# Attention weights times V as high and low fp32r parts on 128 array columns, with masks and one product on GpSimd

## The chip, the cores and the metric

The kernel runs on one core of a Trainium2 chip. The metric is the device time of one execution in microseconds. The engines are named as in the profile: PE is TensorE, DVE is VectorE, ACT is ScalarE, POOL is GpSimd, SP issues most of the DMAs. PEld is the weight load of a matmul, which runs beside the matmul ahead of it.

## The reference

Two layers on 512 tokens of width 1024, everything in float32. Layer 0 mixes by stick-breaking attention with 16 heads of 64 columns, layer 1 by a gated linear recurrence; a squared-ReLU MLP follows each. The change touches the attention alone:

```python
# q, k are RMS-normalised per head; s < t throughout
z = einsum('bhqd,bhkd->bhqk', q, k) * scale
causal = s < t
log_stay = where(causal, log_sigmoid(-z), 0.0)
log_between = cumsum(log_stay, axis=3, reverse=True) - log_stay
weights = where(causal, exp(log_sigmoid(z) + log_between), 0.0)
out = einsum('bhqk,bhkd->bhqd', weights, v)
```

So the weight of key s for query t is sigmoid(z[t,s]) times the product of sigmoid(-z[t,j]) over all j between s and t.

## The kernel before

Activations live transposed, 1024 features in eight tiles of 128 partitions by 512 tokens. Most matrix products are made exact enough by splitting both operands into a high fp32r part and a low remainder and adding three products (high by high, high by low, low by high). Weights come in slabs of 1 MB: two raw tiles `wr` from HBM, ACT casts each to the high part `wh`, DVE subtracts to get the low part `wl`. There are three `wr` buffers, two pairs `wh`, `wl`.

The attention goes by four groups of four heads. For each group the q, k and v projections (`gemm_x`, 96 products of 256 columns each, tile `ps_mm`) run on PE, and the heads of the group run while the next group's projections fill PE. In the last group the filler is the output projection (`gemm_w`, products of 512 columns). The order on PE is written by the program at build time: the class `Line` holds a clock that adds a cost per matmul, a main task (projections) and up to three live tasks (`prepare_pair`, two `head`s); a task yields the planned microseconds until it may go on, from the table `LAG`. The other engines' orders come from a scheduler that follows priorities; instructions wait for each other by semaphores.

A head has four query blocks T = 0 to 3, block T with T + 1 key blocks of 128. `z_of(T)` makes logits `z` on PE; ACT writes `sn` = sigmoid(-z) (two buffers) and `sg` = sigmoid(z); a DVE scan turns `sn` into the running product from the diagonal back; a DVE multiplication joins `sg` and the shifted `sn`. `turn(T)` transposes the blocks on PE into PSUM (`pa`); ACT and DVE bring them to SBUF as `at`, DVE multiplying the diagonal block by the constant `before`, which is the causal mask. `apply(T)` multiplies `at` by the V columns of the head in f32, 64 array columns, one product per key block, ten products per head, into `po`. `po` is one PSUM bank (pool tag `av`, one buffer) that two heads of a pair share, one in the lower and one in the upper 64 partitions. When both are done `split_out` makes the high and low part of the pair's output.

At the start, tile `ps_tr` holds the first k projection; its weights are the second slab.

Of the kernel before, what the change touches and what calls it, by code (L numbers as in the profile page):

```python
# [16 lines left out]
P = 128  # L17
# [13 lines left out]
def level_columns(H, skip):  # L31
# [27 lines left out]
def trunk(  # L59
# [20 lines left out]
    wp = ctx.enter_context(tc.tile_pool(name="wp", bufs=2))  # L80
    ap = ctx.enter_context(tc.tile_pool(name="ap", bufs=2))
# [3 lines left out]
        "P": 16, "Q": 16, "X5": 2, "R4": 4, "B": 2, "qT": 13, "sn": 2, "AT": 3, "sq": 2, "bc": 1,  # L85
# [4 lines left out]
    def sb(tag, shape=(P, S), dt=F32, name=None):  # L90
        return ap.tile(list(shape), dt, tag=tag, bufs=BUFS[tag], name=name or tag)
# [77 lines left out]
    rows = sb("AT", (40, P), name="rows")  # L169
# [6 lines left out]
    def gain(layer, j, kt):  # L176
# [10 lines left out]
    before = cp.tile([P, 2 * P], F32, name="before")  # L187
# [7 lines left out]
    nc.vector.memset(before, 1.0)  # L195
    nc.gpsimd.affine_select(
        out=before[:, P:], in_=before[:, P:], pattern=[[1, P]], compare_op=ALU.is_gt,
        fill=0.0, base=0, channel_multiplier=-1,
    )
    def late_constants():  # L200
        nc.vector.tensor_mul(gqk, gq, gk)
# [45 lines left out]
    def slab_halves(spec):  # L247
# [5 lines left out]
        def load(a):  # L253
            raw = wp.tile([P, h, nc_], F32, tag="wr", bufs=3, name="wr")
# [161 lines left out]
    def attention(norm):  # L416
# [74 lines left out]
        for g in range(4):  # L491
# [27 lines left out]
            vs = []  # L519
            for pair in range(2):  # L520
                shared = {"po": None}
# [4 lines left out]
            V = sb("B", (P, TT, SLAB), name="V")  # L526
            for hf in range(2):
                p = ps("mm")
                for u in range(2):
                    yield from gemm_x(p[:, u * SLAB : (u + 1) * SLAB], wsl, 2 * hf + u, acts)  # L530
                for u in range(2):
                    t = 2 * hf + u
                    nc.scalar.activation(
                        out=V[:, t, :], in_=p[:, u * SLAB : (u + 1) * SLAB], func=AF.Copy,
                        scale=r[:, t : t + 1],
                    )
            vs.append(V)
        return outs, heads

    live = {"sg": 0}  # L540
# [28 lines left out]
    def head(ready, vs, pair, j, shared, outs, slot):  # L569
# [3 lines left out]
        hc = (2 * pair + j) * SB_DH  # L573
# [6 lines left out]
        def z_of(T):  # L580
# [14 lines left out]
            nc.vector.tensor_tensor(  # L595
# [3 lines left out]
        at = [None] * TT  # L599

        def turn(T):
            W = (T + 1) * P
# [3 lines left out]
            at[T] = sb("AT", name="at")  # L606
            lead = W - P if T > 1 else 0
            if lead:
                nc.scalar.copy(at[T][:, :lead], p[:, :lead])
            nc.vector.tensor_mul(at[T][:, lead:W], p[:, lead:W], before[:, 2 * P - (W - lead) :])  # L610

        def apply(T):
            if shared["po"] is None:
                shared["po"] = ps("av", name="po")
            o = blk(shared["po"], T)[j * SB_DH : (j + 1) * SB_DH, :]
            for b in range(T + 1):
                mm(o, vs[0][:, b, hc : hc + SB_DH], blk(at[T], b), b == 0, b == T)

        for step in LAG["head"]:
            if isinstance(step, float):  # L620
                yield step
            else:
                kind, T = step
                while kind == "a" and not vs:
                    yield 0.5
                {"z": z_of, "t": turn, "a": apply}[kind](T)
                if step == ("t", TT - 1):
                    live["sg"] -= 1
        if j == 1:
            outs[slot] = split_out(shared["po"])  # L630
# [304 lines left out]
    def mix(sc, task, V, G, j, outs, slot):  # L935
# [30 lines left out]
        og = sb("AT", name="og")  # L966
# [11 lines left out]
    def store(m, t0, n):  # L978
# [4 lines left out]
        o = sb("AT", name="o")  # L983
# [8 lines left out]
    def trunk_steps():  # L992
# [15 lines left out]
        "raws": [wp.tile([P, KT // 2, SLAB], F32, tag="wr", bufs=3, name="wr") for _ in range(2)],  # L1008
# [17 lines left out]
    gq = sb("AT", (P, SB_DH), name="gq")  # L1026
    gk = sb("AT", (P, SB_DH), name="gk")
    nc.sync.dma_start(out=gq, in_=sb_q_gain.to_broadcast([P, SB_DH]))
    nc.sync.dma_start(out=gk, in_=sb_k_gain.to_broadcast([P, SB_DH]))
# [56 lines left out]
```

## Time and profile before

| what | value |
|---|---|
| three runs | 1322.35, 1324.25, 1326.43 us, median 1324.25 |
| profiled execution | 1325.41 us, span 1323.7 us |
| PE busy | 1300.2 us, 98% of the span |
| DVE busy | 798.7 us, 60% |
| ACT busy | 446.0 us, 34% |
| POOL busy | 80.0 us, 6% |
| f32 products of weights and V (`po`) | 320 records, start 70.8 to 286.7 us |
| HBM | 107.41 MB read, 83 GB/s over the span |

A line of the profile names the source line, the engine, the operation and its tiles (out<-in), the shapes and the count, then busy time, mean length of one in ns, and the idle time ahead of it with what ended it. One f32 matmul is recorded as two instructions, an fp32r matmul as one. In the view by order of time a row begins with its start and its length in us; matmul lengths overlap, so what a matmul costs is read from one start to the next.

### The profile page before, as it was taken

What the parts mean: (1) busy time and instruction counts of PE and PEld (TensorE: products, weight loads), DVE (VectorE), ACT (ScalarE), POOL (GpSimd) and SP (SyncE); (2) the same over time, 40 slices, a digit from 0 to 9 for tenths busy, and PEclk for the clock granted to TensorE, in tenths of its full rate; (3) what the DMA queues carried; (4) which work ended last, traced back from release to release, by engine and by line L of the source; (5) the groups of instructions that cost most, each with busy time, mean ns of one, the idle gap of its engine ahead of it and who ended that gap; (6) DMA issues with size and microseconds to landing.
All of it is one profiled execution on the core that took longest, in us unless ns stands there. A gap on an engine that the chain in (4) does not pass through costs nothing.

```text
span 1323.7 us, 17619 instructions
## 1 busy us (share of the span) xinstructions
PE 1300.2 (98%) x6993; PEld 1104.2 (83%) x6993; DVE 798.7 (60%) x1534; ACT 446.0 (34%) x756; POOL 80.0 (6%) x139
## 2 busy tenths in 40 slices
PE   7999999999999999999999999999999999999998
PEld 7989898778888888888888888888888888888887
DVE  5787687867535435345578888797764353453441
ACT  5554454544212222123333333342432221221221
POOL 0100000000000000000013222232000000000000
PEclk8999999999999999999999999999999999999999
DMA  5312121113333333333321222221333333333331
GB/s 178 108 33 65 33 68 61 49 48 96 96 96 96 96 96 96 96 96 96 96 89 47 88 64 65 64 65 64 96 96 96 96 96 96 95 96 94 97 96 48
DMA packets 110657, 110.64 MB, mean 84 GB/s; under 512 B 3848, under 2 KB 106416, under 8 KB 110576
## 3 DMA queue, kind: packets, MB, share of 16 engines
q1 hardware_dynamic: 110496, 109.22, 26.7%
q8 instruction: 55, 0.90, 0.3%
q0 software_dynamic: 80, 0.31, 0.1%
q14 instruction: 26, 0.21, 0.0%
HBM read 107.41 MB, written 2.10 MB: 83 GB/s over the span
## 4 chain that ended last, share of the span: by engine, by line
PE 84%; DVE 10%; POOL 2%; issue 2%; ACT 1%; SPq 1%; DMA 1%; DVEq 0%; POOLq 0%; ACTq 0%
PE ps_mm L151 70%; PE po L151 3%; PE ps_z L151 3%; POOL tot L812 2%; DVE sc L845 2%; PE ps_s L151 2%; DVE wl L264 2%; PE pa L155 1%; PE z L151 1%; DVE qr L826 1%; PE po_h L151 1%; PE ps_tr L151 1%; DVE sn L591 1%; DVE X L863 1%; DVE X L867 1%
## 5 line engine op out<-in xcount | busy, mean ns | idle before, releaser
L263 ACT CAST wh<-wr 128x1024 fp32r<-128x1024 f32 x198 | 199.8, 1051 | 399.8 <-PE ps_mm L151 367.8
L264 DVE TENSOR_TENSOR wl<-wr,wh 128x1024 fp32r<-128x1024 f32 x198 | 237.7, 1230 | 17.6 <-ACT wh L263 16.8
L151 PE MATMUL ps_mm<-xh,wh 128*128 128x512 f32 x592 | 232.1, 392 | 0.0
L151 PE MATMUL ps_mm<-xh,wl 128*128 128x512 f32 x592 | 230.5, 389 | 0.0
L151 PE MATMUL ps_mm<-xl,wh 128*128 128x512 f32 x592 | 230.5, 389 | 0.0
L151 PE MATMUL ps_mm<-hh,wh 128*128 128x512 f32 (+1 forms) x520 | 204.1, 393 | 0.0
L151 PE MATMUL ps_mm<-hh,wl 128*128 128x512 f32 (+1 forms) x520 | 203.6, 392 | 0.0
L151 PE MATMUL ps_mm<-hl,wh 128*128 128x512 f32 (+1 forms) x520 | 203.5, 391 | 0.0
L151 PE MATMUL ps_mm<-wh,xh 128*128 128x256 f32 x592 | 173.6, 293 | 0.0
L695 DVE TENSOR_TENSOR xT<-xT,ps_mm 128x512 f32<-128x512 f32 x63 | 43.4, 688 | 213.2 <-PE ps_mm L151 213.2
L151 PE MATMUL ps_mm<-wl,xh 128*128 128x256 f32 x592 | 167.8, 283 | 3.1 <-DVE wl L459 3.1
L151 PE MATMUL ps_mm<-wh,xl 128*128 128x256 f32 x592 | 167.6, 283 | 0.0
L151 PEld LDWEIGHTS ps_mm<-xh,wl 128*128 128x128 f32 x592 | 111.1, 188 | 23.2
L151 PEld LDWEIGHTS ps_mm<-xh,wh 128*128 128x128 f32 x592 | 111.2, 188 | 22.7
L151 PEld LDWEIGHTS ps_mm<-xl,wh 128*128 128x128 f32 x592 | 111.2, 188 | 22.5
L151 PEld LDWEIGHTS ps_mm<-wh,xh 128*128 128x128 f32 x592 | 113.5, 192 | 4.2 <-issue 3.6
L151 PEld LDWEIGHTS ps_mm<-wl,xh 128*128 128x128 f32 x592 | 113.6, 192 | 3.9 <-DVE wl L459 3.3
L151 PEld LDWEIGHTS ps_mm<-hh,wl 128*128 128x128 f32 x520 | 97.6, 188 | 22.9
L151 PEld LDWEIGHTS ps_mm<-hl,wh 128*128 128x128 f32 x520 | 97.7, 188 | 22.7
L151 PEld LDWEIGHTS ps_mm<-hh,wh 128*128 128x128 f32 x520 | 97.7, 188 | 22.6
L672 DVE SCALAR_TENSOR_TENSOR u<-ps_mm,R 128x512 f32<-128x512 f32 x60 | 41.5, 692 | 123.1 <-PE ps_mm L151 123.1
L151 PEld LDWEIGHTS ps_mm<-wh,xl 128*128 128x128 f32 x592 | 113.5, 192 | 0.0
(213 smaller groups left out, 1653.6 us busy)
## 6 DMA issues: line engine op xcount, KB each, us to landing
wr<-in_mlp_w_dram SPq DMA_DIRECT2D x128, 512.0 KB, 3.7
wr<-in_hg_w_in_dram SPq DMA_DIRECT2D x32, 512.0 KB, 3.8
wr<-in_sb_w_qkv_dram SPq DMA_DIRECT2D x22, 512.0 KB, 3.5
wr<-in_sb_w_o_dram SPq DMA_DIRECT2D x8, 512.0 KB, 3.9
wr<-in_hg_w_o_dram SPq DMA_DIRECT2D x8, 512.0 KB, 3.7
xin<-in_x_dram SPq DMA_DIRECT2D x8, 256.0 KB, 5.3
out_dram<-o SPq DMA_DIRECT2D x7, 256.0 KB, 2.3
wr<-in_sb_w_qkv_dram SPq DMA_DIRECT2D x4, 256.0 KB, 5.5
```

The lines of the kernel that those rows point to most:

```text
L151: nc.tensor.matmul(o, lhsT=lhsT, rhs=rhs, start=start, stop=stop, **kw)
L155: nc.tensor.transpose(o, in_, ident)
L263: nc.scalar.copy(hi[:, c, :], raw)
L264: nc.vector.tensor_tensor(out=lo[:, c, :], in0=raw, in1=f(hi[:, c, :]), op=ALU.subtract)
L591: nc.vector.tensor_tensor_scan(out=rev, data0=rev, data1=later[:, S - W :][:, ::-1], initial=1.0, op0=ALU.mult, op1=ALU.max,)
L672: nc.vector.scalar_tensor_tensor(out=u, in0=p, scalar=0.0, in1=norm.R, op0=ALU.max, op1=ALU.mult)
L695: nc.vector.tensor_add(xT[m], xT[m], p)
L812: nc.gpsimd.tensor_tensor(out=tots[H][:, :, None], in0=t0, in1=t1, op=ALU.mult)
L826: nc.vector.tensor_tensor(out=q1, in0=q1, in1=t0.to_broadcast([P, S // (2 * H), H]), op=ALU.mult)
L845: nc.vector.copy_predicated(out=o, mask=mask.rearrange("p (g w) -> p g w", g=g)[:, None].to_broadcast([P, 2, g, w]), data=data.rearrange(" ...
L863: nc.vector.tensor_tensor(out=o, in0=qv[:, :, :, part * H : part * H + w], in1=tv[:, :, :, part - 1, None].to_broadcast([P, TT, g, w]), op ...
L867: nc.vector.tensor_tensor(out=C, in0=B[:, :, :, H:], in1=tv[:, :, :, 1, None].to_broadcast([P, TT, g, wc]), op=ALU.mult,)
```

## The change

1. The products of weights and V take fp32r operands. `turn` writes the transposed blocks twice, `ath` (ACT cast) and `atl` (DVE remainder), for two query blocks together: half 0 holds T = 0 and 1, half 1 holds T = 2 and 3, interleaved so that one product of 256 columns serves both queries of a half. V is kept as high and low part side by side, so that a head's weight is 128 columns: the high part's sums come out in the lower 64 partitions, the low part's in the upper. Twelve products per head: eight of 256 columns, four of 128.
2. `gather`, new: each head has its own `po`; ACT copies one half of the partitions to `sum`, DVE adds the other. A pair's two heads meet in `sum`, and `split_out` reads that.
3. The causal mask is an `affine_select` on GpSimd, and the multiplication of `sg` and `sn` is on GpSimd as well. The constant `before` is gone.
4. V of a group is written in two tiles of a pool with two buffers; the main task waits for the older group's heads (`yield older`) before it makes the next V. `wr` has two buffers instead of three. The tiles `ath`, `atl` of each half have one pair of buffers (`live[half]` lets one head at a time use it).
5. `LAG` has `z`, `t`, `tt`, `a` instead of the list `head`.

```diff
-    "head": [
-        ("z", 0), 0.46, ("z", 1), 2.26, ("z", 2), 1.2, ("t", 0), ("z", 3), 1.5, ("t", 1), ("a", 0),
-        1.54, ("t", 2), ("a", 1), 1.58, ("t", 3), ("a", 2), 1.37, ("a", 3),
-    ],
+    "z": (0.46, 2.26, 1.8),
+    "t": (5.2, 5.0, 4.8, 4.8),
+    "tt": 0.7,
+    "a": (1.6, 2.1),
...
-            raw = wp.tile([P, h, nc_], F32, tag="wr", bufs=3, name="wr")
+            raw = wp.tile([P, h, nc_], F32, tag="wr", bufs=2, name="wr")
...
+            yield older
...
+                    vh, vl = v[:, u, :, 0, :], v[:, u, :, 1, :]
+                    nc.scalar.activation(out=vh, in_=src, func=AF.Copy, scale=r[:, t : t + 1])
+                    nc.vector.scalar_tensor_tensor(
+                        out=vl, in0=src, scalar=r[:, t : t + 1], in1=f(vh), op0=ALU.mult,
+                        op1=ALU.subtract,
                     )
...
-            nc.vector.tensor_tensor(
+            nc.gpsimd.affine_select(
+                out=sg[:, W - P :], in_=sg[:, W - P :], pattern=[[-1, P]], compare_op=ALU.is_gt,
+                fill=0.0, base=0, channel_multiplier=1,
+            )
+            nc.gpsimd.tensor_tensor(
                 out=sg[:, : W - 1], in0=sg[:, : W - 1], in1=sn[:, 1:W], op=ALU.mult
             )
...
+            nc.scalar.copy(ah, src)
+            nc.vector.tensor_tensor(out=al, in0=src, in1=f(ah), op=ALU.subtract)
+
+        def apply(half):
+
+            if not half:
                 shared["po"] = ps("av", name="po")
...
+            n, to = 2 * half + 2, 2 * P * (1 - half)
+            for b in range(n):
+                w = 1 if b == n - 1 else 2
+                for i, t in enumerate(at[half]):
+                    mm(
+                        shared["po"][:, to : to + w * P], vs[0][b // 2][:, b % 2, 2 * pair + j],
+                        t[:, 2 * b : 2 * b + w, :], b + i == 0, b == n - 1 and i == 1,
+                    )
+
+        def gather():
+
+            if j == 0:
+                shared["sum"] = sb("qT", name="sum")
+            po, to = [
+                t.rearrange("p (t q) -> p t q", q=P) for t in (shared["po"], shared["sum"])
+            ]
+            nc.scalar.copy(to[own], po[other][:, ::-1, :])
+            nc.vector.tensor_tensor(out=to[own], in0=po[own][:, ::-1, :], in1=to[own], op=ALU.add)
...
+        turned = 0.0
+        for T in range(TT):
+            yield from until(max(done[T] + LAG["t"][T], turned + LAG["tt"]))
+            half = T // 2
+            if T % 2 == 0:
+                while live[half]:
+                    yield 0.2
+                live[half] = 1
+            turn(T)
+            if T == 2:
+                yield from until(turned + LAG["a"][0])
+                yield from finish(0)
+            turned = line.at
+        live["sg"] -= 1
+        yield from until(turned + LAG["a"][1])
+        yield from finish(1)
+        gather()
         if j == 1:
-            outs[slot] = split_out(shared["po"])
+            outs[slot] = split_out(shared["sum"])
```

What this makes of the order shows at two places. The first is PE in group one, where the first head of a pair ends and the second goes on. Before (`po_941` belongs to both heads; `pa` are transposes, `z` logits, `ps_mm` projections):

```order
L151 MATMUL po_941<-at_999,V_576 64x128 x4
L155 MATMUL pa_1033<-ident_67,sg_845 128x128 x4
L151 MATMUL po_941<-at_1009,V_576 64x128 x3
L151 MATMUL z_1044<-kst_778,qh_780 128x256
L151 MATMUL z_1044<-kst_778,ql_782 128x256
L151 MATMUL ps_mm_918<-wh_709,xh_233 128x256
```

Now, with `po_968` the first head's bank and `po_1065` the second's:

```order
L153 MATMUL po_968<-ath_964,V_706 128x256
L153 MATMUL po_968<-atl_965,V_706 128x256
L153 MATMUL po_968<-ath_964,V_706 128x128
L153 MATMUL po_968<-atl_965,V_706 128x128
L157 MATMUL pa_1057<-ident_70,sg_848 128x128 x3
L153 MATMUL po_1065<-ath_984,V_624 128x256
L153 MATMUL po_1065<-atl_985,V_624 128x256
L153 MATMUL po_1065<-ath_984,V_624 128x128
```

The second head's first products stand three transposes behind the first head's last; before, both wrote parts of one tile. The same bank is meant by both names, so `po_1065` waits for the `gather` of `po_968`.

The second place is the end of group one on PE, where the fourth head ends. Before, with `ps_mm_1234` the next group's projection:

```order
L151 MATMUL ps_mm_1234<-wh_908,xl_280 128x256
L151 MATMUL ps_mm_1234<-wh_908,xh_156 128x256
L151 MATMUL ps_mm_1234<-wl_909,xh_156 128x256
L151 MATMUL ps_mm_1234<-wh_908,xl_157 128x256
L151 MATMUL po_1151<-at_1276,V_576 64x128 x4
L151 MATMUL ps_mm_1234<-wh_908,xh_165 128x256
```

Now the main task waits for the group's heads, and nothing else stands there (`po_1188` is the third head's bank, `po_1298` the fourth's):

```order
L153 MATMUL po_1188<-atl_1185,V_706 128x256
L153 MATMUL po_1188<-ath_1184,V_706 128x128
L153 MATMUL po_1188<-atl_1185,V_706 128x128
L157 MATMUL pa_1290<-ident_70,sg_1092 128x128 x3
L153 MATMUL po_1298<-ath_1213,V_624 128x256
L153 MATMUL po_1298<-atl_1214,V_624 128x256
L153 MATMUL po_1298<-ath_1213,V_624 128x128
L153 MATMUL po_1298<-atl_1214,V_624 128x128
L157 MATMUL pa_1303<-ident_70,sg_1092 128x128 x4
L153 MATMUL po_1298<-ath_1294,V_624 128x256
```

Projections no longer stand between the last transposes and the last products. On DVE at that place, before (`rq` belongs to the next group's norm, `wl` to a weight split):

```order
L610 TENSOR_TENSOR at_1243<-pa_1238,before_89 128x128
L228 TENSOR_SCALAR rq_a_1209<-mqk_1205 128x32
L264 TENSOR_TENSOR wl_1224<-wr_1225,wh_1223 128x1024
L610 TENSOR_TENSOR at_1253<-pa_1249,before_89 128x128
L232 TENSOR_SCALAR rq_y_1208<-rq_a_1209 128x32
L264 TENSOR_TENSOR wl_1224<-wr_1229,wh_1223 128x1024
L610 TENSOR_TENSOR at_1276<-pa_1271,before_89 128x128
```

and now, with `sum_1287` the add of `gather` for the third head:

```order
L501 SCALAR_TENSOR_TENSOR mqk_1251<-ss_711,em_428 128x16
L260 TENSOR_TENSOR wl_1270<-wr_1271,wh_1269 128x1024
L620 TENSOR_TENSOR atl_1295<-pa_1290,ath_1294 128x3x128
L643 TENSOR_TENSOR sum_1287<-po_1188,sum_1287 64x512
L224 TENSOR_SCALAR rq_a_1255<-mqk_1251 128x32
L260 TENSOR_TENSOR wl_1270<-wr_1275,wh_1269 128x1024
L228 TENSOR_SCALAR rq_y_1254<-rq_a_1255 128x32
L233 TENSOR_TENSOR rq_a_1255<-rq_y_1254 128x32
L234 SCALAR_TENSOR_TENSOR rq_a_1255<-rq_a_1255,mqk_1251 128x32
L237 SCALAR_TENSOR_TENSOR rq_y_1254<-rq_a_1255,rq_y_1254 128x32
L620 TENSOR_TENSOR atl_1295<-pa_1303,ath_1294 128x4x128
```

The add for the third head stands behind a weight split and the fourth head's remainder `atl_1295`, and the remainder of its last block behind a second split. On ACT the copies of that place stand behind a Square and a cast of weights:

```order
L422 ACTIVATE sqq_1247<-ps_mm_1106 128x512
L259 CAST wh_1269<-wr_1271 128x1024
L642 COPY sum_1287<-po_1188 64x512
L619 CAST ath_1294<-pa_1290 128x3x128
L259 CAST wh_1269<-wr_1275 128x1024
L619 CAST ath_1294<-pa_1303 128x4x128
```

The copy of `po_1188` moved in behind `sqq` and `wh`, ahead of the fourth head's cast.

More of the change, by code (lines that the diff above doesn't have):

```diff
@@ L167, in trunk @@
     nc.scalar.copy(ones_r, ones)
-    rows = sb("AT", (40, P), name="rows")
+    rows = sb("H0", (40, P), name="rows")
     nc.sync.dma_start(out=rows[0:32, :], in_=norm_gains.rearrange("l j (k p) -> (l j k) p", p=P))
@@ L572, in head @@
         kst, qh, ql = shared["k"][j], shared["q"][j], shared["ql"][j]
-        hc = (2 * pair + j) * SB_DH
+        own, other = [slice(i * SB_DH, (i + 1) * SB_DH) for i in (j, 1 - j)]
         while live["sg"] >= BUFS["X5"]:
@@ L619, in head @@
[L619 to L628, printed above, removed]
+            if T % 2 == 0:
+                at[half] = [
+                    sb(f"H{half}", (P, 4 * half + 3, P), dt=F32R, name=n) for n in ("ath", "atl")
+                ]
@@ new lines, in until @@
+        def until(t):
+            while t > line.at:
+                yield t - line.at
+        done = []
+        for T in range(TT):
+            z_of(T)
+            done.append(line.at)
+            if T + 1 < TT:
+                yield LAG["z"][T]
+        turned = 0.0
+        for T in range(TT):
+            yield from until(max(done[T] + LAG["t"][T], turned + LAG["tt"]))
+            half = T // 2
+            if T % 2 == 0:
+                while live[half]:
[6 more added lines that the diff above has]
+            turned = line.at
```

63 lines of the change are left out of this document (28 added, 35 removed).

## The prediction

> **What bounds the kernel now.** I read the page's busy times first, then a table of stretches over the attention stage, then the waits of the matmul engine, then its instructions in order of time. The first two say that TensorE (PE) carries the time:
>
> ```profile
> PE 1300.2 (98%) x6993; PEld 1104.2 (83%) x6993; DVE 798.7 (60%) x1534; ACT 446.0 (34%) x756; POOL 80.0 (6%) x139
> ```
>
> ```profile
> 53.00:111.00 58.00, 56.84 (x434) 50.95 (x433) 46.75 (x89) 30.35 (x67) 2.09 (x4) 1.00 0.18 55
> 111.00:175.00 64.00, 62.84 (x484) 57.01 (x482) 46.90 (x89) 31.33 (x67) 2.09 (x4) 1.00 0.16 50
> 175.00:233.00 58.00, 56.84 (x433) 50.97 (x432) 46.76 (x89) 30.36 (x67) 1.56 (x3) 1.00 0.16 55
> 233.00:300.00 67.00, 65.19 (x342) 50.24 (x341) 50.59 (x86) 32.99 (x66) 0.00 (x0) 0.97 0.15 48
> ```
>
> Each row is one group of four heads with its projections: length, then busy PE, weight loads, DVE, ACT, POOL. Of 247 us PE idles 1.16 + 1.16 + 1.16 + 1.81 = 5.3 us. DVE is busy 191.0 us of the same 247, so it has little room when something must be prompt. The waits of PE name the cause of most idleness, the logits waiting for ACT to free a PSUM buffer:
>
> ```profile
> PE z L151 <- ACT sg L589: 3.2, 3, 1.2
> ```
>
> A PE instruction that gets shorter here is therefore worth its length, and one that waits costs its wait, since PE's order is fixed and all later filler stands behind it.
>
> **Products of weights and V.** PE in order of time (start, length, count):
>
> ```profile
> 99.15 0.28 PE L151 MATMUL ps_mm<-wh,xl 128*128 128x256 f32 x1
> 99.36 1.09 PE L151 MATMUL po<-at,V 128*64 128x128 f32 x8
> 100.38 0.39 PE L151 MATMUL ps_mm<-wh,xh 128*128 128x256 f32 x1
> 100.60 0.28 PE L151 MATMUL ps_mm<-wl,xh 128*128 128x256 f32 x1
> 100.72 0.28 PE L151 MATMUL ps_mm<-wh,xl 128*128 128x256 f32 x1
> 100.84 0.60 PE L155 MATMUL pa<-ident,sg 128*128 128x128 f32 x4
> 101.37 0.87 PE L151 MATMUL po<-at,V 128*64 128x128 f32 x6
> 102.17 0.39 PE L151 MATMUL ps_mm<-wh,xh 128*128 128x256 f32 x1
> ```
>
> An f32 product is two records: eight take 1.02 us from start to start, six 0.80, so 0.13 each. A head has ten products, 20 records, 2.60 us; sixteen heads 41.6 us. The new head issues twelve fp32r products, eight of 256 columns and four of 128. A 256-column fp32r product takes 0.12 us (100.60 to 100.72). No row shows 128 fp32r columns. Below lies half of 0.12, if columns alone count; above lies the f32 price of two records, 0.26. I take 0.12, since each product brings a full 128-column weight load and the f32 transposes, of the same 128 by 128 shape, take 0.13 (four from 100.84 to 101.37). Then a head costs 1.44 us, all 23.0: a gain of 18.6 us (22.4 at the low end, 9.6 at the high one). The Trainium skill, "TensorE: Matmul & The Clock Gate", section "Back-to-back issue gap", gives about 81 ns per product for a stream of loads and 128-column products; it would add 2.5 us to the gain, an estimate from that page.
>
> A change of kind costs too: 0.21 instead of 0.12 before the f32 products (99.15 to 99.36), 0.22 instead of 0.12 behind them (100.38 to 100.60). By the order, 16 of the 64 runs of products of weights and V followed fp32r work, 16 x 0.09 = 1.4 us, which go; returns from f32 to fp32r fall from 72 to 69, 0.3 us. Together 1.7 us.
>
> **The wait that comes in.** One bank holds `po`. Before, two heads shared it and nobody read it between them. Now each head takes it anew, and its first product waits until ScalarE has copied one half of the last head's sums and VectorE has added the other (`gather`). Prices:
>
> ```profile
> L610 DVE TENSOR_TENSOR at<-pa,before 128x128 f32<-128x128 f32 x48 | 13.5, 285 | 17.9 <-ACT at L609 16.8 <-PE pa L155 0.9
> L560 DVE TENSOR_TENSOR kst<-pk,kst 64x512 fp32r<-64x512 f32 x16 | 11.0, 689 | 15.0 <-ACT kst L558 14.6
> L595 DVE TENSOR_TENSOR sg<-sg,sn 128x511 f32<-128x511 f32 x16 | 11.0, 687 | 0.6
> ...
> L237 DVE TENSOR_TENSOR rq_a<-rq_y 128x32 f32<-128x32 f32 x12 | 2.3, 191 | 0.3
> ```
>
> ```profile
> L558 ACT CAST kst<-pk 64x512 fp32r<-64x512 f32 x16 | 9.3, 580 | 6.1 <-PE pk L155 5.0 <-DVE kst L560 0.9
> ...
> L609 ACT COPY at<-pa 128x384 f32<-128x384 f32 x16 | 7.7, 481 | 26.9 <-PE pa L155 26.7
> ```
>
> ```profile
> 105.16 0.39 PE L151 MATMUL ps_mm<-wh,xh 128*128 128x256 f32 x1
> ...
> 105.26 0.59 ACT L340 CAST oh<-po 128x512 fp32r<-128x512 f32 x1 [3.31 <-PE po L151]
> ...
> 105.88 0.69 DVE L341 TENSOR_TENSOR ol<-po,oh 128x512 fp32r<-128x512 f32 x1 [0.38 <-ACT oh L340]
> ```
>
> The last rows give the handovers: ACT starts 0.10 behind PE, DVE 0.03 behind ACT; back to PE I put 0.05, an estimate from these two. The plain takeover is 0.10 + 0.58 (copy) + 0.03 + 0.69 (add) + 0.05 = 1.45 us, and PE has only three transposes to fill it (the order in the part on the change), 0.40: a wait of 1.05. Going through the built orders I find it five times: 5.3 us. Twice VectorE has the new head's remainder queued ahead of the add (three blocks: 0.29 for one, 0.69 for four, so 0.55); with the cast of 0.48 ahead of that, 0.10 + 0.58 + 0.48 + 0.03 + 0.55 + 0.69 + 0.05 - 0.40 = 2.1 in the fourth group, and 1.9 in the second, where the chain starts only at the transposes: 4.0 us. Two takeovers have over 2 us of filler and cost nothing.
>
> The first and third group end without filler. With the page's prices of a weight split,
>
> ```profile
> L263 ACT CAST wh<-wr 128x1024 fp32r<-128x1024 f32 x198 | 199.8, 1051 | 399.8 <-PE ps_mm L151 367.8
> L264 DVE TENSOR_TENSOR wl<-wr,wh 128x1024 fp32r<-128x1024 f32 x198 | 237.7, 1230 | 17.6 <-ACT wh L263 16.8
> ```
>
> ACT reaches the copy only behind a Square (some 0.60, as the 0.59 cast) and a cast of 1.05, and DVE has a 1.23 split and the 0.55 remainder ahead of the add: 0.10 + 0.60 + 1.05 + 1.23 + 0.55 + 0.69 + 0.05 = 4.3 from the last filler, less 0.96 of products and 0.40 of transposes, 2.9 us. Then the four-block transposes must become `ath` and `atl` with another split and five operations of 0.19 ahead: (0.95 + 1.23 + 0.69) less 1.0 of PE work, 1.85. Two such ends: 9.5 us. At the stage's end the final head's sums pass copy, add, cast, remainder, behind two splits, against nine 512-column products:
>
> ```profile
> 286.97 22.59 PE ps_mm L151 x96
> ```
>
> They last 9 x 0.235 = 2.1 us; with 0.96 of last products PE could go on at 3.1, the cast ends at 0.10 + 1.05 + 2 x 1.23 + 0.69 + 0.59 = 4.9, and its remainder 0.7 later: 2.4 us. New waits together 5.3 + 4.0 + 9.5 + 2.4 = 21.2 us. They could lie 10 lower if VectorE is early everywhere, or 5 higher if its queue is long.
>
> **GpSimd.** It takes 64 masks and 64 multiplications.
>
> ```profile
> L818 POOL TENSOR_TENSOR kk<-kk,tot 128x256 f32<-128x256 f32 x48 | 37.1, 773 | 74.6 <-PE ps_s L151 72.7
> ...
> masks.py:199 POOL TENSOR_SCALAR_AFFINE_SELECT ident<-ident 128x128 f32<-128x128 f32 x1 | 0.3, 293 | 0.1
> ```
>
> By 773 ns for 256 columns a head's 1276 columns (127, 255, 383, 511) are 3.9 us, the masks 1.2: 5 us per head of some 14, so GpSimd keeps up, and the planned time from logits to transposes, now about 5 us, holds its longest pair, 0.3 + 1.5, with 3 us for the steps ahead of it. VectorE loses the products (0.29 to 0.69, 1.9 us per head) and four mask multiplications (1.3), and gains remainders of all ten blocks (about 1.9) and the add (0.69): nearly even. But GpSimd disturbs it:
>
> ```profile
> 704.37 1.61 DVE L264 TENSOR_TENSOR wl<-wr,wh 128x1024 fp32r<-128x1024 f32 x1
> ...
> 707.44 1.23 DVE L264 TENSOR_TENSOR wl<-wr,wh 128x1024 fp32r<-128x1024 f32 x1
> ```
>
> ```profile
> 703.40 1.51 POOL L818 TENSOR_TENSOR kk<-kk,tot 128x256 f32<-128x256 f32 x2 [3.32 <-PE ps_s L151]
> ```
>
> The same split took 0.38 us more while GpSimd's pair ran. If half of 64 products do that, VectorE loses 12 us; between nothing and 24 (all of them), I put a third of 12, 4 us, on PE's path, as VectorE has 56 us free. The Trainium skill's "GPSIMD Engine Reference", section "1. Specifications", says that the two share their SBUF interface and contend where VectorE reads two SBUF operands; the rows agree, and it speaks against this move.
>
> **One raw buffer fewer.** A raw weight tile lands 3.5 us after its issue and is split within 2.3; a slab lasts 11.5 us, so the long stages lose nothing. Only the start does: the second half of slab two now waits for the second starting tile.
>
> ```profile
> 25.47 0.68 DVE L459 TENSOR_TENSOR wl<-wr,wh 128x512 fp32r<-128x512 f32 x1
> ```
>
> ```profile
> wr<-in_sb_w_qkv_dram SPq DMA_DIRECT2D x22, 512.0 KB, 3.5
> ```
>
> ```profile
> 29.57 11.52 PE ps_tr L151 x96
> ```
>
> Free at 26.15, landed at 29.7, split at 31.95; PE wants it twelve products after 29.57, at 31.1: about 1.0 us (0 to 3). The sixteen remainders of V on VectorE I cost at nothing: V is needed only after the next slab's 11.5 us; without that cover each would cost its 0.4 us. ScalarE's extra copies, some 1.5 us per head, fit into the 122 us that it idles in these stretches.
>
> **Sum.** From the profiled execution's 1325.4 us: - 18.6 - 1.7 + 21.2 + 1.0 + 4.0 = 1331.3. That execution lies 1.2 above the median, so 1330 us. About 0.3% is what a measurement can tell from no change.
>
> **Rivals.** First, relief: VectorE's queue gets short at the right places, since the product between scan and transposes leaves it. Then nothing stands ahead of the adds: each group end falls from 4.75 to about 2.5, the two late takeovers to 1.05, the stage's end to nothing, 8.8 us, and the old 5.3 us idle goes: 1316 us, faster. It decides where adds start 0.03 behind their copies everywhere. For it: the even VectorE balance; against: the built order puts splits ahead. Second, VectorE saturates: all 24 us of disturbance come, and two thirds of them fall on the path, since no room is left: 1330 - 4 + 16 = 1342, slower. It decides where DVE is busy above 95% of these stretches. Third, 128 fp32r columns cost two records: 64 x 0.14 = 9 us more, 1339.
>
> **Chances.** My forecast 0.50 (own range 1322 to 1338), relief 0.22, saturation 0.18, dear narrow products 0.10. Slower holds 0.30 of the first, saturation and 0.08 of the last: 0.56, given as 0.55; the same 0.18 and 0.02, 0.20; the rest, 0.25, faster. The range reaches from relief with cheap narrow products (1316 - 4, drawn in to 1314) to saturation and a little over, 1345.
>
> **What would show it.** Twelve `po` products near 1.44 us per head; PE waits of `po` on DVE's `sum`, 1 us and more, some ten times, and of `po` on `atl` at two group ends; DVE scans and splits above 1.22 us; one wait near 31 us. Wrong if `po` hardly waits for `sum`, or if DVE's mean times rise by half.

## The result, and the profile after

The changed kernel takes 1336.65 us (median of five runs, 1333.68 to 1340.06); the kernel before, beside it, 1324.25 (1321.63 to 1326.43). The ratio is 1.0098, 95% interval 1.0071 to 1.0124: 12.4 us slower. Forecast were 1330, 1314 to 1345, and "slower" with 0.55. The profiled execution took 1340.06 us with a span of 1338.3, against 1325.41 and 1323.7; the sums below are between these two, 14.65 us apart. One execution stands apart from all others here: the profiled one of the run e3 took 2547.24 us, with PE's products nearly twice as far from one another from end to end, so that e3 is read by its other four alone.

The page's busy times and the stretches of the four groups (length, busy PE, weight loads, DVE, ACT, POOL, then PE's granted clock, DMA share, GB/s; the first row starts at 41 us where the prediction's starts at 53, and from 41 us on PE idled the same 1.16 us before):

```profile
PE 1280.0 (96%) x6865; PEld 1108.9 (83%) x6865; DVE 806.6 (60%) x1501; ACT 466.1 (35%) x804; POOL 171.0 (13%) x266
```

```profile
41.00:111.00 70.00, 59.87 (x433) 57.14 (x433) 57.32 (x106) 38.02 (x81) 24.05 (x36) 0.89 0.24 76
111.00:175.00 64.00, 54.42 (x404) 51.62 (x404) 41.42 (x63) 32.56 (x74) 27.25 (x36) 0.93 0.11 34
175.00:233.00 58.00, 51.24 (x400) 49.42 (x400) 46.19 (x75) 33.22 (x74) 20.57 (x31) 0.97 0.18 56
233.00:300.00 67.00, 55.44 (x321) 48.95 (x320) 49.51 (x85) 34.06 (x76) 25.29 (x38) 0.87 0.15 48
```

PE was busy in nearly all of these stretches before and is not now. The column that the prediction never used is the clock: 0.87 to 0.97, where it was 0.97 to 1.00. What PE waited for in the first 330 us (total, times, longest; `atl` is the remainder of a head's own blocks):

```profile
PE po L153 <- DVE sum L643: 12.4, 7, 4.0
PE po L153 <- DVE atl L620: 7.8, 8, 1.6
PE po L153 <- DVE rq_a L224: 6.2, 2, 3.1
PE ps_mm L153 <- DVE xT L692: 4.2, 1, 4.2
...
PE po L153 <- ACT ath L619: 3.0, 3, 1.6
PE ps_mm L153 <- ACT oh L336: 1.7, 1, 1.7
```

The two waits put down to `rq_a` are takeovers as well, those at the two group ends: `rq_a` is what VectorE does right behind the add (the add starts at 102.73, `rq_a` at 103.33, PE goes on at 103.55). So the takeovers cost 12.4 + 6.2 us.

One of the plain takeovers, and what follows it, in PE's order of time (start, length):

```profile
80.93 0.38 PE L153 MATMUL po<-atl,V 128*128 128x256 f32 x1 [1.65 <-DVE atl L620]
...
81.51 0.28 PE L153 MATMUL po<-atl,V 128*128 128x256 f32 x1
81.62 0.22 PE L153 MATMUL po<-ath,V 128*128 128x128 f32 x1
81.68 0.28 PE L153 MATMUL po<-atl,V 128*128 128x128 f32 x1
81.80 0.51 PE L157 MATMUL pa<-ident,sg 128*128 128x128 f32 x3
83.35 0.58 PE L153 MATMUL po<-ath,V 128*128 128x256 f32 x1 [1.04 <-DVE sum L643]
...
84.58 0.41 PE L153 MATMUL ps_mm<-wl,xh 128*128 128x256 f32 x1
84.80 0.41 PE L153 MATMUL ps_mm<-wh,xl 128*128 128x256 f32 x1
...
90.15 0.28 PE L153 MATMUL ps_mm<-wh,xh 128*128 128x256 f32 x1
90.27 0.28 PE L153 MATMUL ps_mm<-wl,xh 128*128 128x256 f32 x1
```

The wait is 1.04 us, 2.4 us behind another of 1.65. Behind it the same 256-column product takes 0.22 us from start to start (84.58 to 84.80), at 90.15 again 0.12. The five-microsecond windows there say why:

```profile
80.00:85.00 5.00, 3.03 (x17) 2.79 (x18) 2.03 (x4) 1.06 (x2) 1.35 (x3) 0.73 0.23 79
85.00:90.00 5.00, 5.00 (x25) 4.87 (x25) 2.78 (x5) 2.80 (x8) 2.26 (x4) 0.59 0.00 0
...
100.00:105.00 5.00, 1.87 (x11) 1.67 (x11) 4.93 (x11) 2.75 (x4) 1.64 (x4) 0.78 0.28 83
105.00:110.00 5.00, 4.18 (x18) 3.49 (x17) 3.96 (x11) 1.16 (x2) 0.00 (x0) 0.50 0.38 127
```

From 85 to 90 PE is busy for all of 5.00 us, and has 25 matmul records, where the same window of before has 39 (an f32 product counts twice there): the profile's busy time hides this loss. Over the windows of 5 us from 40 to 340, PE's idle time rose from 5.3 to 40.9 us, and busy time multiplied by what the clock lacks to 1.0 rose from 1.7 to 19.7 us.

One more difference lies where nothing was said to change. Behind the attention (from the first `ps_st` to the end of the span) the kernel takes 997.3 us, before 1008.2. The groups by shape of the MLP, before and after, both from 345 to 640 us, where the changed kernel comes later and has fewer of them:

```profile
L151 PE MATMUL ps_mm<-hh,wh 128*128 128x512 f32 x222 | 87.7, 395 | 0.0
```

```profile
L153 PE MATMUL ps_mm<-hh,wh 128*128 128x512 f32 x192 | 74.7, 389 | 0.0
```

Each product that streams a Q tile (`hh`, `hl`) is 6 ns shorter by its record, 7 ns from start to start (0.2333 and 0.2267 us on the mean between 380 and 640 us). The changed kernel has a pool `gp` of its own for the tiles P and Q, which neither the change's list nor the prediction spoke of.

### The profile page after: what moved, and what is told of

Same layout as the page of the kernel before. It is cut to its first block, busy times and chain, and to the rows that moved or that the text cites. A ratio compares the mean times of both kernels' runs of the same rounds, so it can differ in the third digit from the quotient of the medians.

```text
span 1338.3 us, 17547 instructions
## 1 busy us (share of the span) xinstructions
PE 1280.0 (96%) x6865; PEld 1108.9 (83%) x6865; DVE 806.6 (60%) x1501; ACT 466.1 (35%) x804; POOL 171.0 (13%) x266
## 4 chain that ended last, share of the span: by engine, by line
PE 80%; DVE 12%; POOL 3%; issue 3%; ACT 2%; SPq 1%; DMA 0%; POOLq 0%; DVEq 0%; ACTq 0%
PE ps_mm L153 68%; PE ps_z L153 3%; DVE wl L260 2%; POOL tot L861 2%; DVE sc L894 2%; PE po L153 2%; DVE sn L593 2%; PE ps_s L153 2%; DVE qr L875 1%; PE po_h L153 1%; PE z L153 1%; PE pa L157 1%; POOL sg L601 1%; DVE X L912 1%; PE ps_tr L153 1%
## 5 line engine op out<-in xcount | busy, mean ns | idle before, releaser
L260 DVE TENSOR_TENSOR wl<-wr,wh 128x1024 fp32r<-128x1024 f32 x198 | 237.6, 1230 | 17.4 <-ACT wh L259 17.0
L153 PE MATMUL ps_mm<-hh,wh 128*128 128x512 f32 (+1 forms) x520 | 201.3, 387 | 0.0
L153 PE MATMUL ps_mm<-hh,wl 128*128 128x512 f32 (+1 forms) x520 | 200.7, 386 | 0.0
L153 PE MATMUL ps_mm<-hl,wh 128*128 128x512 f32 (+1 forms) x520 | 200.6, 386 | 0.0
L153 PE MATMUL ps_mm<-wh,xh 128*128 128x256 f32 x592 | 176.9, 299 | 0.4 <-DVE V L534 0.4
L153 PE MATMUL ps_mm<-wl,xh 128*128 128x256 f32 x592 | 170.5, 288 | 3.0 <-DVE wl L455 3.0
L153 PE MATMUL ps_mm<-wh,xl 128*128 128x256 f32 x592 | 170.4, 288 | 0.0
L153 PEld LDWEIGHTS ps_mm<-xl,wh 128*128 128x128 f32 x592 | 111.2, 188 | 22.4
L153 PEld LDWEIGHTS ps_mm<-wl,xh 128*128 128x128 f32 x592 | 116.6, 197 | 3.3 <-DVE wl L455 3.2
L153 PEld LDWEIGHTS ps_mm<-wh,xh 128*128 128x128 f32 x592 | 116.6, 197 | 2.1 <-DVE V L534 0.7
L153 PEld LDWEIGHTS ps_mm<-wh,xl 128*128 128x128 f32 x592 | 116.4, 197 | 0.0
```

What stands on the lines that cost most here:

```text
L153: nc.tensor.matmul(o, lhsT=lhsT, rhs=rhs, start=start, stop=stop, **kw)
L260: nc.vector.tensor_tensor(out=lo[:, c, :], in0=raw, in1=f(hi[:, c, :]), op=ALU.subtract)
```

## The experiments

Theory: what came in is a wait per head and, behind waits, half the clock; what came out is the work of the products and, through the new pool, 7 ns on each Q product. Rivals: VectorE paces the stage, so that any gain on PE is waited away; GpSimd's slow products make the heads late. Ratios are to the kernel before, run beside each.

**The pool, done alone and undone.** e1 is the kernel before with `gp`, e2 the changed kernel without it.

```diff
+    gp = ctx.enter_context(tc.tile_pool(name="gp", bufs=16))
...
-        return ap.tile(list(shape), dt, tag=tag, bufs=BUFS[tag], name=name or tag)
+        pool = gp if tag in "PQ" else ap
+        return pool.tile(list(shape), dt, tag=tag, bufs=BUFS[tag], name=name or tag)
```

> The kernel before, with one edit: the activation tiles of tags P and Q (hidden layer and attention outputs among them) come from a pool of their own, as in the changed kernel. Nothing else of the change. My theory: the products that take these tiles as moving operand go from 0.235 to 0.227 us each because the tiles lie at other addresses; the two MLPs and the output projections get 10 to 12 us shorter, so about 1313 us against 1324. Rival: the changed kernel's later stages are shorter for another reason (the third raw weight buffer gone, or the attention's work), then this is 1324 within 2.

> The changed kernel with the tags P and Q back in the shared pool. My theory: it loses what the pool gave, 10 to 12 us, so about 1347 us, which is what the rest of the change costs: +23 us on the kernel before. Rival: addresses do not matter, then 1337 as the changed kernel.

e1 took 1311.99 us (ratio 0.9915, 0.9896 to 0.9934), e2 1346.59 (1.0183, 1.0159 to 1.0208). The pool is worth 12 us in the one and 10 in the other: without it the change costs 22.9 us, not 12.4, and with it alone the kernel before is faster than the changed one by 25.

**The takeover.** e3 gives `po` two banks, taken from the transposes; e4 takes that bank from the transposes alone.

```diff
-    PB = {"mm": 2, "z": 2, "tr": 3, "av": 1}
+    PB = {"mm": 2, "z": 2, "tr": 2, "av": 2}   # e4: "av": 1
```

> The changed kernel with two PSUM banks for the heads' sums (po) and two instead of three for transposes, so that a head's first product need not wait for the gather of the head before. Takeover theory: the waits of po on VectorE's add (12 us, and the 6 us charged to rq_a at two group ends) go, and the clock drops behind them go too: 15 to 25 us faster than the same kernel with one bank and two transpose banks (e4), 1315 to 1322 if the lost transpose bank costs nothing. Rival (VectorE is simply late everywhere): the waits move to atl and ath, and the time falls by less than 6 us.

> Control for e3: the changed kernel with two instead of three PSUM banks for transposes, po unchanged. Both theories: 1337 to 1345, new waits of transposes on ath and atl at most 8 us.

e3 took 1327.81 us (median of four; 1.0036, 1.0022 to 1.0050), e4 1345.72 (1.0167, 1.0149 to 1.0185): at equal transposes the second bank saves 17.9 us. In e4 the takeovers' waits are 12.4 us for `sum` and 6.3 for `rq_a`, 18.7 together, about what the second bank saved. The granted clock rose too, from 0.983 to 0.986 in e4 to 0.988 to 0.992 in e3; how the gain splits between waits and clock is not shown, since the only trace of e3 is of the execution set apart above. And a bank costs 9 us where it is taken away.

**The waits filled with useless work.** e5 puts products that nobody reads ahead of ten of the waits.

```diff
+    KEEP = {
+        (0, 1): 5, (1, 0): 3, (3, 0): 11, (3, 1): 2, (6, 0): 14, (8, 1): 5, (9, 0): 3, (11, 0): 11,
+        (11, 1): 2, (13, 0): 11,
+    }
...
+            n = KEEP.get((2 * slot + j, half), 0)
+            if n:
+                p = ps("tr", name="keep")
+                for _ in range(n):
+                    nc.tensor.matmul(p[:, 0:P], lhsT=ones, rhs=ones, start=True, stop=True)
             apply(half)
```

> The changed kernel with 67 useless f32 products of 128 columns (0.26 us each at full clock, 17.4 us in all) put on PE ahead of ten places at which the changed kernel's PE waited (1.65, 1.04, 3.13, 0.68, 4.02, 1.65, 1.04, 3.12, 0.68 and 3.22 us, 20.2 us together); the order is otherwise the same and the products' results are not used. Clock theory (PE's clock falls because PE stood still): the products take the place of the waits and cost about 2 us beside them, and of the 19.7 us that the lower clock cost between 40 and 340 us some 16 come back: 1337 + 2 - 16 = 1323, between 1318 and 1328, with granted clocks of 0.9 and more in the windows that stood at 0.5 to 0.75. Rival (the clock falls for another reason, or the stage is paced by VectorE and every gain is waited away): 1336 to 1342.

1327.67 us (1.0032, 1.0019 to 1.0045): 9.0 us less with 17.4 us more work. The windows that stood at 0.5 to 0.8:

```profile
80.00:85.00 5.00, 4.10 (x33) 3.71 (x33) 2.42 (x4) 1.41 (x4) 1.46 (x4) 1.00 0.30 97
85.00:90.00 5.00, 3.81 (x29) 3.39 (x27) 4.09 (x7) 4.04 (x11) 3.41 (x6) 1.00 0.02 3
...
100.00:105.00 5.00, 3.76 (x29) 3.21 (x28) 4.86 (x12) 2.13 (x4) 0.52 (x2) 1.00 0.40 118
105.00:110.00 5.00, 5.00 (x43) 5.00 (x44) 4.62 (x9) 1.20 (x2) 0.00 (x0) 1.00 0.28 95
```

All at 1.00. The loss by the clock fell from 19.7 to 4.5 us; of the 20.2 us of idle time that was filled, 14.0 stayed away (40.9 to 26.9) and 6 came back as other waits. So the clock falls because PE stands still, and it is a cost of its own. VectorE takes a part of the gain back, not all of it.

**Filler where the waits are.** e6 moves the wait for the older heads behind the next group's products, so that the ends of the first and third group have filler. e7 adds a planned distance between a head's `gather` and the next head's first product.

```diff
-            yield older
-            V = []
+            V, got = [], []
             for hf in range(2):
                 p = ps("mm")
+                got.append(p)
                 for u in range(2):
                     yield from gemm_x(p[:, u * SLAB : (u + 1) * SLAB], wsl, 2 * hf + u, acts)
+            yield older
+            for hf, p in enumerate(got):
...
-    "a": (1.6, 2.1),                      # e7 only, from here
+    "a": (1.8, 2.2),
+    "p": 1.8,
...
+            if not half:
+                yield from until(live["po"] + LAG["p"])
...
         gather()
+        live["po"] = line.at
```

> The changed kernel in which the main task makes both halves of the next V in PSUM (96 products) before it waits for the older group's heads, instead of waiting first; so the first and third group's last head has filler. The two ends stood for 3.13 + 0.68 and 3.12 + 0.68 us of waits, 7.6. If only the waits count: 1337 - 7.6 = 1329. If the clock behind them counts as well (about 4.4 us from 100 to 115 and 3.4 from 235 to 250): 1321. If VectorE paces the stage, the time stands again in other waits: 1334 to 1338.

> The kernel of e6_filler_at_ends in which, besides, the planner knows the takeover: a head's first product of weights and V is planned at least 1.8 us behind the last head's gather, and the planned time from transposes to products is 1.8 and 2.2 us instead of 1.6 and 2.1. By the order, 13 of 15 takeovers then have 2.2 us of PE work ahead of them instead of 0.4. PE idled 40.9 us between 40 and 340 us in the changed kernel and lost 19.7 to its clock. If waits and clock both go where they are covered: idle about 12 and clock about 5, so 1337 - 43 = 1294, between 1288 and 1302. If only the waits go: 1308. If VectorE paces the stage (it is busy some 225 of these 300 us, against 190 of 247 in the best stretches of before): above 1320.

e6 took 1320.18 us (0.9971, 0.9962 to 0.9981), as the clock theory had it, though not quite by the waits named: the takeover at the first end still waits 2.41 us instead of 3.13, but nothing follows it. At the third group's end 2.78 us are still waited, and the clock is 0.50 for some 6 us behind them.

```profile
100.00:105.00 5.00, 4.67 (x39) 4.70 (x40) 4.69 (x15) 0.59 (x1) 0.00 (x0) 1.00 0.69 211
105.00:110.00 5.00, 5.00 (x44) 5.00 (x43) 3.55 (x6) 2.05 (x4) 0.00 (x0) 1.00 0.01 3
```

e7 took 1305.96 us (0.9875, 0.9856 to 0.9893), the best of all: 18 us under the kernel before, 31 under the changed one, 6 under e1. Its waits of `po` in the whole stage:

```profile
PE po L154 <- DVE atl L623: 9.1, 9, 2.1
...
PE po L154 <- DVE sum L646: 1.5, 2, 0.8
```

The waits for `sum` are gone, those for the remainder are not, and the loss by the clock is 4.4 us. I had expected 1294. The stage from 41 us to the first `ps_st`, of before and of e7:

```profile
41.00:316.00 275.00, 269.71 (x1857) 234.18 (x1856) 213.75 (x397) 136.92 (x281) 5.81 (x12) 0.99 0.20 61
```

```profile
41.00:307.00 266.00, 243.39 (x1725) 224.01 (x1725) 218.65 (x364) 156.52 (x329) 99.99 (x140) 0.98 0.20 63
```

DVE is busy 218.65 of 266 us, 82%. The clock came as expected (4.4 us lost, 5 expected); the waits did not, PE still idles 22.6 us instead of 12. Of these, 14.5 end at a VectorE instruction, 9.1 of them at remainders, and 7.6 at a ScalarE one, so VectorE's queue is a part of what is left and not all of it. The 1308 of "only the waits go" lies near the time, but there the clock's loss would have stayed.

**The product back on VectorE.** e8 is the changed kernel with one word changed; the masks stay on GpSimd.

```diff
-            nc.gpsimd.tensor_tensor(
+            nc.vector.tensor_tensor(
                 out=sg[:, : W - 1], in0=sg[:, : W - 1], in1=sn[:, 1:W], op=ALU.mult
```

> The changed kernel with the product of sg and sn back on VectorE; the masks stay on GpSimd. VectorE gets 64 products, 30 us together at the lengths of before (0.29 to 0.69), and loses the disturbance, some 5 us by its scans (512 columns 1277 against 1220 ns, 128 columns 546 against 416). If VectorE's room is what the adds and remainders lack, PE waits longer for sum and atl: 1345 to 1360. If GpSimd's long products (1.3 us) and the disturbance are what makes the heads late: below 1333. Within 1334 to 1344 where it runs by was not on the path.

1340.64 us (1.0127, 1.0110 to 1.0144), 4.0 more than the changed kernel: nearly a draw, as the third case had it. The scans of 512 and of 128 columns, changed kernel and e8, and the waits of `po` for `sum` in e8:

```profile
L593 DVE TENSOR_TENSOR_SCAN sn<-sn,later 128x512 f32<-128x512 f32 x16 | 20.4, 1277 | 9.9 <-ACT sn L590 9.9
...
L593 DVE TENSOR_TENSOR_SCAN sn<-sn,later 128x128 f32<-128x128 f32 x16 | 8.7, 546 | 0.3 <-ACT sn L590 0.2
```

```profile
L593 DVE TENSOR_TENSOR_SCAN sn<-sn,later 128x512 f32<-128x512 f32 x16 | 19.9, 1242 | 4.9 <-ACT sn L590 4.9
...
L593 DVE TENSOR_TENSOR_SCAN sn<-sn,later 128x128 f32<-128x128 f32 x16 | 7.0, 439 | 0.1
```

```profile
PE po L153 <- DVE sum L643: 16.2, 10, 4.3
```

GpSimd's products do slow VectorE's scans (439 to 546 ns), but with them on VectorE the adds come later still (16.2 against 12.4 us). The two intervals overlap (1.0071 to 1.0124 and 1.0110 to 1.0144), so the move to GpSimd gains little, if anything.

**Waits made on purpose.** e10 is e1 with 16 waits in the first MLP, where PE otherwise never stands.

```diff
+    def stand(q):
+        p = ps("av", name="first")
+        nc.tensor.matmul(p, lhsT=ones, rhs=later, start=True, stop=True)
+        slow = sb("R4", name="slow")
+        with tc.high_priority(offset=AHEAD):
+            nc.scalar.copy(slow, p)
+            for _ in range(STAND[q]):     # 1, 2, 4, 8
+                nc.scalar.copy(slow, slow)
+        p = ps("av", name="then")
+        nc.tensor.matmul(p[:, 0:P], lhsT=ones, rhs=slow[:, 0:P], start=True, stop=True)
```

> The kernel of e1_before_own_pool, whose PE hardly waits and runs at a clock of 0.999, with 16 waits made in the first MLP, one every second slab: a useless f32 product of 512 columns, a chain of 2, 3, 5 or 9 copies of 512 columns on ScalarE (0.59 us each, four waits of each kind), and a product of 128 columns that reads the end of it. By the copies the waits are 1.3, 1.9, 3.1 and 5.5 us, more where a weight cast comes between: 47 us together, and the added products some 20. If waiting costs only itself: 1312 + 47 + 20 = 1379 and a granted clock of 1.0 behind each. If a wait of some 3 us halves the clock for about 5 us and one of 1 us leaves it alone (as the changed kernel's trace suggests): eight waits lose 2 to 5 us each, 1395 to 1420, and the windows behind the long ones show 0.5.

1429.65 us (1.0806, 1.0781 to 1.0832). The waits came out longer than planned, 67.6 us in all (2.13 to 7.55), so that without a clock 1312 + 68 + 20 = 1400 would stand there. One of the shortest kind and the longest, and the windows of 1 us from their ends on:

```profile
348.46 0.65 PE L666 MATMUL then<-slow,ones 128*128 128x128 f32 x2 [2.52 <-ACT slow L664]
...
759.98 0.80 PE L666 MATMUL then<-slow,ones 128*128 128x128 f32 x2 [7.55 <-ACT slow L664]
```

```profile
348.46:349.46 1.00, 1.00 (x4) 0.90 (x5) 0.90 (x2) 0.00 (x0) 0.00 (x0) 0.59 0.88 281
349.46:350.46 1.00, 1.00 (x4) 0.81 (x3) 0.00 (x0) 0.00 (x0) 0.00 (x0) 0.50 0.95 249
...
351.46:352.46 1.00, 1.00 (x5) 0.81 (x4) 0.00 (x0) 0.00 (x0) 0.00 (x0) 0.70 0.75 257
352.46:353.46 1.00, 1.00 (x6) 0.83 (x5) 0.00 (x0) 0.00 (x0) 0.00 (x0) 1.00 0.09 27
```

```profile
759.98:760.98 1.00, 1.00 (x3) 0.93 (x4) 0.00 (x0) 0.00 (x0) 0.00 (x0) 0.50 0.00 0
...
763.98:764.98 1.00, 1.00 (x4) 0.80 (x3) 0.00 (x0) 0.00 (x0) 0.00 (x0) 0.50 0.06 16
764.98:765.98 1.00, 1.00 (x6) 0.82 (x5) 0.00 (x0) 0.00 (x0) 0.00 (x0) 0.96 0.00 0
```

Behind every one of the 16 the clock is 0.5 for 3 to 6 us, however long the wait was, which costs 1.5 to 2.8 us more each, 31 us together: 1400 + 31 against 1430 measured.

**Where the 7 ns come from.** e9 (first edit) keeps the pool but makes it last, so that its tiles lie high in SBUF; e12 (second) is e2, with no pool, and 128 unused bytes ahead of the first Q tile.

```diff
-    gp = ctx.enter_context(tc.tile_pool(name="gp", bufs=16))
     ap = ctx.enter_context(tc.tile_pool(name="ap", bufs=2))
+    gp = ctx.enter_context(tc.tile_pool(name="gp", bufs=16))
...
+    pads = []
+
     def split_out(p):
+        if not pads:
+            pads.append(ap.tile([P, 32], F32, tag="pad", bufs=1, name="pad"))
+            nc.gpsimd.memset(pads[0], 0.0)
```

> The changed kernel with its own pool for the tiles P and Q made last instead of ahead of the general pool: same pools, buffers and order, only other SBUF addresses. The sixteen Q tiles then lie at bytes 195456 to 226176 of a partition (changed kernel: 112000 to 142720; before: 194304 to 227072), the sixteen P tiles at 162688 to 193408 (79232 to 109952; before about 111000 to 142000). Address theory (a 512-column product is slower when its moving tile lies high): products from hh take 395 ns again instead of 389 and the time goes back to that of e2_after_shared_pool, 1347; 20 us more than that if the P tiles are high enough too. Rival (a pool of their own spares waits or order): unchanged, 1334 to 1340, and 389 ns.

> The kernel of e2_after_shared_pool (1347, no pool of its own) with an unused tile of 128 bytes per partition made ahead of the first Q tile: all Q tiles, and the tile bc behind them, lie 128 bytes further on (193408 to 224128 instead of 193280 to 224000), nothing else moves. In the runs so far the 512-column products from hh took 395 ns where Q tiles start at a multiple of 256 bytes (before 194304, e2 193280) and 389 where they start at an odd multiple of 128 (changed kernel 112000, e1 117120, e9 195456). Alignment theory: 389 ns, 0.2265 us from product to product, and the 10 us come back: 1337, between 1333 and 1341. Rival (the pool as such: its buffers, waits or order): 395 ns and 1343 to 1351.

e9 took 1336.40 us (1.0102, 1.0071 to 1.0133), unchanged: "slower where it lies high" fell. e12 took 1337.92 (1.0100, 1.0070 to 1.0130): 8.7 of the 10 us between e2 (1346.59) and the changed kernel came back without a pool. The MLP's products in e2, e9 and e12:

```profile
L151 PE MATMUL ps_mm<-hh,wh 128*128 128x512 f32 x192 | 75.8, 395 | 0.0
```

```profile
L153 PE MATMUL ps_mm<-hh,wh 128*128 128x512 f32 x192 | 74.7, 389 | 0.0
```

```profile
L151 PE MATMUL ps_mm<-hh,wh 128*128 128x512 f32 x192 | 74.7, 389 | 0.0
```

In these kernels a 512-column fp32r product takes 395 ns where its moving tile starts at a multiple of 256 bytes (Q tiles of before and e2) and 389 where it starts at an odd multiple of 128 (Q tiles of the changed kernel, e1, e9 and e12). The P tiles start at an odd multiple of 128 in all six, and the first MLP's products from them (`xh`, `xl`) took 389 ns in all six. The pool had moved the Q tiles from the one kind of address to the other.

**A version on top of e7** that did not pay: 16 useless products at the last two heads, and the last logits of each head planned 1 us later.

```diff
-    "z": (0.46, 2.26, 1.8),
+    "z": (0.46, 2.26, 2.8),
...
+    KEEP = {(14, 1): 12, (15, 0): 2, (15, 1): 2}
```

> The kernel of e7_filler_everywhere with 16 useless f32 products (0.26 us each) where the last two heads of the stage still wait 2.35 + 1.58, 0.73 and 0.68 us, and the fourth block's logits planned 1 us later (z 2.8 instead of 1.8), since they waited 1.51, 1.13, 1.16 and 0.52 us for ScalarE. The clock lost 4.4 us behind the first, which should come back to 1; of the 4.3 us before the logits half is gained if nothing moves behind them. 1306 - 3 - 2 = 1301, between 1298 and 1306. If VectorE paces the stage: 1306 again or a little more.

1308.83 us (0.9897, 0.9873 to 0.9922), against 1301 expected, no better than e7. The loss by the clock did fall, to 1.4 us, but the filler waited itself, for the transposes' bank that it was given:

```profile
270.88 4.57 PE L658 MATMUL keep<-ones 128*128 128x128 f32 x24 [3.84 <-DVE atl L624]
```

Whether the later logits helped or hurt, these two edits together do not tell.

## Why the prediction held, point by point

The sign, the range and most single terms held; that the sum came near is luck. Two terms that were not in it, +18.0 and -12.1, largely cancel: without the pool the same change took 1346.59 us (e2), above the range's end of 1345. In the profiled executions:

| term | predicted | measured |
|---|---|---|
| products, kind switches and what else PE no longer does | -20.3 | -26.0 |
| PE's idle time in the stage | +21.2, and 4.0 for VectorE disturbed | +35.6 (5.3 to 40.9) |
| clock behind the waits | not in the sum | +18.0 (1.7 to 19.7) |
| address of the Q tiles | not in the sum | -12.1 (10.9 behind the stage, 1.2 in it) |
| start | +1.0 | -0.9 (first `pk` at 51.6 instead of 52.5; it lies between 50.5 and 56.5 in the other traces but e3's) |
| sum | +5.9 | +14.6 |

The measured work is what is left of the stage from first `pk` to first `ps_st` without idle time and clock loss: 315.0 - 54.3 - 5.9 = 254.8 us in e1, whose Q tiles are fast too, and 289.4 - 40.9 - 19.7 = 228.8 in the changed kernel.

- **Narrow products.** Taken at 0.12 us; the rows show 0.06 for the first (81.62 to 81.68) and 0.12 for the second, so that a head costs about 1.3 us and not 1.44. That is 2 us of the 5.7 by which the work shrank more than predicted. The rest shows at the transposes, which the sum had left alone: from start to start all of them took 22.4 us in e1 and 16.5 in e7, more than is missing; what goes the other way has no row. In the order of before, 48 runs of f32 products stood directly behind transposes, and three transposes ahead of such a run took 0.41 to 0.49 us; ahead of fp32r work three took 0.24 to 0.27. The prediction priced the change between fp32r and f32 work and not this one.
- **The plain takeover.** 1.05 us, five times, was predicted; 1.04, five times, is in the trace (83.35, 146.38, 168.92, 219.16 and 303.57). The chain copy, add, product was right to the last handover.
- **Late takeovers and ends.** Two late takeovers were put at 4.0 us and came to 3.22 + 4.02; two ends at 4.75 each and came to 3.13 + 0.68 and 3.12 + 0.68; the stage's end at 2.4, measured 1.67 + 0.23. Together with the plain ones 21.2 predicted and 21.9 measured; single ones were off by a factor of two and more (the late takeover of the second group 4.02 for 1.9, the ends' second waits 0.68 for 1.85). The 14 us of idle time on top are places I had not gone to: `po` waiting for the remainder `atl` of its own head (1.65 twice, 0.89 twice, 1.0 twice), for a cast 1.61, and an output product for `xT`, 4.19. All but the cast are VectorE being late: it comes to each of these remainders straight from a scan (at 80.21 from one that began at 79.60).
- **The start.** The wait near 31 us, put at 1.0, came: 0.86 at 30.40. It does not show in the table, since the first `pk` moves by more than that from run to run.
- **GpSimd.** Its disturbance of VectorE, put at 4 us of cost, exists (scans of 128 columns 416 ns before, 546 after), but undoing the move costs 4.0 us rather than giving 4 back (e8), with intervals that overlap. The Trainium skill's "GPSIMD Engine Reference", section "1. Specifications", was right on the contention; that it speaks against the move was my reading, and the measurement does not bear it out.
- **The step that failed** is the sentence that a PE instruction "that waits costs its wait". It costs its wait and, often, half clock behind it. The view of stretches that the prediction quotes has a column for the clock, 0.97 in the last row of before, the one with the most idle time. The length of a wait alone does not decide. All 16 of e10 were followed, from 2.13 us up, and 1.65 and 1.04 us at 81 us in the changed kernel, 2.4 us apart; but 2.41 us in e6, 3.06 in the kernel before (at 19.93 us) and 3.23 in e4 (at 142.93 us) left the clock at 1.00. The same waits can go either way: 1.61 and 1.02 us left it at 1.00 in the changed kernel (137 us) and halved it in e5 (132 us); 0.85 and 0.96 us halved it in the kernel before (248 and 250 us) and left it alone in e1. The Trainium skill's "TensorE: Matmul & The Clock Gate", section "What's actually happening", has the rule: half rate after an idle window of about 3.4 us, full rate after a busy one. The length of the slow stretch agrees, about one or two such windows (3 to 6 us in e10); the idle time does not, as 2.13 us were enough. The Trainium skill's same section has the window run freely, so that equal waits can fall into it differently; this would fit if a part of a window is enough, but no run here shows the window itself.
- **Relief, saturation, dear narrow products.** None of the three rivals came, though two lie nearer to the time (1342 and 1339) than the forecast's 1330. The place for saturation was DVE busy above 95% of the stretches; it is 57.32 of 70 us, 82%, in the fullest.

## What to carry to other kernels

A wait on TensorE can have two prices, its length and a slow stretch behind it, which follows often and not always; to find the second, read the clock column of short windows, since the busy time counts slow work as work. A new wait that stands some ten times on a full engine is worth a look at the planner before it is worth a faster instruction: the same edit went from 1.0% slower to 1.2% faster by moving one wait and planning one distance (e7). The 1.2% includes what the pool gives by itself; against e1, which has the pool alone, e7 is 6 us faster. And a difference where nothing was changed is a finding: compare like groups of instructions in the stages that should be equal.

## What the hardware showed that was not expected

Half clock followed all 16 waits of 2.13 to 7.55 us that were made in a full stream, for 3 to 6 us whatever the wait's length (e10), yet waits of 2.41, 3.06 and 3.23 us elsewhere were followed by none (e6, before, e4), and equal waits in two runs went either way. In the changed kernel the five runs stand in the order of their granted clock, 0.990 for a span of 1331.9 us to 0.981 for 1338.3. And 128 bytes of offset on the tiles that 512-column fp32r products stream are worth 6 ns on each record, 9 to 12 us of this kernel (e1, e2, e12).
